# RWKV layer: the decays' products alternate between the two halves of the rows, and the scan's gram products run head by head in a fixed order

## The chip, the cores and the metric

The kernel runs on one core of one Trainium2 chip. Its engines work side by side: TensorE (matmuls, PE in the profile; PEld is its weight loads), VectorE (DVE), ScalarE (ACT), GpSimd (POOL) and SyncE (SP), which here only issues DMA transfers. The metric is the device time of one execution in microseconds, and of several executions the median.

## The reference

Two decoder layers over 1024 positions of width 1024. Layer 0 mixes tokens with an RG-LRU, layer 1 with RWKV-7 time mixing; each has a cross-attention and a squared-ReLU MLP behind it. The change lies in layer 1's time mixing alone (16 heads of 64):

```python
xx = x_prev - x
r = (x + xx * mu[0]) @ w_rkv[0]
xw = x + xx * mu[1]
k = (x + xx * mu[2]) @ w_rkv[1]
v = (x + xx * mu[3]) @ w_rkv[2]
xa = x + xx * mu[4]
...
w_log = -jax.nn.softplus(-(w0 + jnp.tanh(xw @ w1) @ w2)) - 0.5
decay = jnp.exp(-jnp.exp(w_log))
a = jax.nn.sigmoid(a0 + (xa @ a1) @ a2)
...
def step(state, inp):
    r_t, w_t, k_t, v_t, a_t, b_t = inp
    sa = jnp.einsum('bhij,bhj->bhi', state, a_t)
    state = (state * w_t[:, :, None, :] + sa[..., None] * b_t[:, :, None, :]
             + v_t[..., None] * k_t[:, :, None, :])
    y_t = jnp.einsum('bhij,bhj->bhi', state, r_t)
    return state, y_t
```

The scan over positions is computed in 16 chunks of 64 positions: products within a chunk are matmuls, and only the state goes from chunk to chunk.

## The kernel before

All large products are made in three matmuls of a split operand (`mm3`, lines 317 to 319: high x high, high x low, low x high), each of at most 128 x 512 outputs into one PSUM bank.

The order on each engine is made by a scheduler that simulates the program; code is not simply run in the order in which it is written. Two helpers narrow it: `self.line(name)` keeps everything issued under one name in the order of writing on each engine, and `self.behind()` puts what follows behind all that was given before. SP issues its transfers strictly in its own order, and each waits for its operands there.

The RWKV layer has these stages in the profile:
- The low-rank products, then eight turns of k products (`fphase` with `w_rkv[0, 1]`), one feature block f of 128 (two heads) each; the last turn has two. Beside turn i the decays of the next block are made by `decay(f)`: the rank-64 outputs for `w2` lie on rows 0 to 63, those for `a2` on rows 64 to 127 of the same tiles (`wa2`, `hwa`), so each of these matmuls uses one half of the rows. Both halves of the positions (`hf`) are made, so there are twelve 64-row matmuls of 512 columns for each f, and a tanh on ACT (L1266) takes each bank.
- Behind turn f, `gram(f)` makes products of the chunk's keys (L1341), masks them on DVE (L1342), and SP stores them (L1348, L1349). From two such blocks POOL solves triangular systems (`solve`, L1369 and L1371, q = 0, 1, 2; DVE has q = 3). `solve_store` copies a part on ACT (L1381) and SP stores both (L1382, L1383).
- The r products: `rwkv_make_mix` makes their inputs (ACT L1156, DVE L1159, then the split of L232 on ACT and L233 on DVE). Each weight block is loaded by SP (L248) and split in the same two lines. Then the v products, with the prefetch for the scan.
- The scan. Ahead of it, the grams, masks and keys of chunks 0 and 1. For chunk c: `values` (L1717, copied on ACT by L1719), `from_state` (L1729), `flip_out` of an earlier chunk (PE L1663, DVE L1668), `solved` (PE L1735, DVE L1737), `scan_gram(c + 1, 0)` (L1612), `update` (PE L1742, DVE L1744), `scan_keys` (L1636), the masks (DVE L1622) and `scan_gram(c + 1, 1)`, `output` (L1749), `post_norm(c - 1)` (DVE L1656), which the next chunk's `flip_out` reads. On POOL run `decayed` (L1724), `scan_scale` (L1602) and the power of `post_var` (L1651). Each of these functions runs under `self.line("scan")`, so their order among each other is fixed on each engine, and the order within one is the scheduler's.

A scan gram has eight matmuls, four head pairs q with two heads h. Head 0 has its operands on rows 0 to 63, head 1 on rows 64 to 127, and the two write to two banks. In the trace each shows as two passes, so 16 rows.

Of the kernel before, what the change touches and what calls it, by code (L numbers as in the profile page):

```python
# [1200 lines left out]
def rwkv(self, X, xt, lw_wa, lw_g, post):  # L1201
    nc, I = self.nc, self.I
    mm = nc.tensor.matmul
# [17 lines left out]
    wa2 = self.split(raw)  # L1221
    xk, xr, xv = ([[], []] for _ in range(3))
    for hf in range(2):
        o = hf * 512
        for lw, sh, hid in maps:
            ps = [self.bank() for _ in range(2)]
# [10 lines left out]
        if hf:  # L1237
            h = maps[0][2]
            nc.scalar.activation(h[0:64, :], h[0:64, :], AF.Tanh)
            hwa = self.split(h)  # L1240
        self.catch_up()
        rwkv_make_mix(self, X, 2, hf, xk[hf])
    h = maps[1][2]
# [10 lines left out]
    hr = [slice(0, 64), slice(64, 128)]  # L1254
    dk, st_k, mg, sol, ld, sm, xts = {}, {}, {}, {}, {}, {}, {}

    def decay(f):
        cs = slice(f * 128, f * 128 + 128)
        c1 = lambda t: t[:, f:f + 1]
        lw, a = self.unit(), self.unit()  # L1260
        for t, r, b in ((lw, slice(0, 64), self.w0h), (a, slice(64, 128), self.a0h)):
            for hf in range(2):
                s = slice(hf * 512, hf * 512 + 512)
                p = self.bank()
                self.mm3(p, (wa2[0][r, cs], wa2[1][r, cs]), (hwa[0][r, s], hwa[1][r, s]), True, True)
                nc.scalar.activation(t[:, s], p, AF.Tanh, bias=c1(b), scale=0.5)  # L1266
        nc.vector.tensor_scalar(lw, lw, -LC, -LC, ALU.mult, ALU.add)
        if f > 1:
            nc.scalar.activation(a, a, AF.Copy, scale=0.5, bias=0.5)
        else:  # L1270
            nc.vector.tensor_scalar(a, a, 0.5, 0.5, ALU.mult, ALU.add)
        IP = self.unit()
        nc.vector.tensor_tensor_scan(IP, d01, lw, 0.0, ALU.mult, ALU.add)
        P = lw
        nc.scalar.activation(P, IP, AF.Exp)
        nc.scalar.activation(IP, IP, AF.Exp, scale=-1.0)
        nc.sync.dma_start(Pd[cs, :], P)
        nc.scalar.copy(self.pc.rearrange("p (c q) -> p c q", q=8)[:, :, f], P[:, 63::64])
        dk[f] = a, P, IP
# [151 lines left out]

    self.depth, self.ahead = DA
    decay(0)
    for i, fs in enumerate(TURNS):
        for f in TURNS[i + 1] if i < 6 else []:
            decay(f)
        if len(fs) > 1:

            self.later.append(lambda: rwkv_make_mix(self, X, 0, 0, xr[0], range(2)))
        if i:  # L1440
            sums(fs[0] - 1)
        self.fphase(I["b_w_rkv"][0, 1], fs, xk, prep)
        if 0 < i < 6:
            gram(fs[0] - 1)
        aside(i)
# [158 lines left out]
    def scan_gram(c, g):  # L1604

        if c >= 16:
            return
        s = cst[c]
        s["pv", g] = [self.bank(h).rearrange("p (q w) -> p q w", q=4) for h in range(2)]
        for q in range(4):  # L1610
            for h in range(2):
                mm(s["pv", g][h][:, q, :], s["st"][g][hr[h], q].rearrange("p w t -> p (w t)"), s["mv"][hr[h], 4 * g + q],  # L1612
                   start=True, stop=True)

    def scan_mask(c, g):
        if c >= 16:
# [70 lines left out]
    for c in range(2):  # L1687
        scan_scale(c)
        for g in range(2):
            scan_gram(c, g)  # L1690
            scan_mask(c, g)
            scan_keys(c, g)
# [4 lines left out]
    for c in range(16):  # L1697
# [5 lines left out]
        s = cst[c]  # L1703
        sv, mv, pcc, xtc, pcs = s["sv"], s["mv"], s["pcc"], s["xt"], s["pcs"]
# [60 lines left out]
        if c:  # L1765
            todo += [(scan_gram, c + 1, 0)]
        if c < 15:
            todo += [(update, 0), (update, 1)]
        if c:
            todo += [(scan_keys, c + 1, 0), (scan_keys, c + 1, 1), (scan_mask, c + 1, 0), (scan_gram, c + 1, 1), (scan_mask, c + 1, 1)]  # L1770
# [6 lines left out]
        if c > 4 and c % 2:  # L1777

            n = (c - 3) // 2
# [8 lines left out]
    w = I["b_w_o"][0]  # L1788
# [54 lines left out]
```

## Time and profile before

| | |
|---|---|
| time, median of 3 runs | 2927.56 us (2922.16 to 2934.81) |
| span of the profiled execution | 2923.2 us |
| mean granted TensorE clock | 0.988 |
| 64-row matmuls of the decays, L317 to L319 | 32 each, 13.6 + 11.7 + 11.7 us busy |
| scan grams, L1612 | 512 passes, 47.4 us busy |

The profile gives no time of its own for the profiled execution beside its span, which runs from the first instruction to the last; the three runs shown lie from 1.0 us below it to 11.6 us above.

In rows of the order of time, the first two numbers are the start in us from the span's start and the duration of the (merged) row, then come engine, line, operation, output<-inputs by their tiles' names without numbers, sizes and a count; in brackets stands how long the engine had been idle and whose work ended that. A row of several instructions lasts from the start of the first to the end of the last. Matmuls are pipelined, so rows overlap by the part of a matmul that is only its way through the array.

### The profile page before, as it was taken

How to read it: one execution, taken by the hardware profiler on the slowest of the kernel's cores; microseconds unless marked ns; L12 is line 12 of the kernel's file. 1: busy time of each engine (PE TensorE's matmuls, PEld its weight loads, DVE VectorE, ACT ScalarE, POOL GpSimd, SP SyncE). 2: the span in 40 equal slices, each digit the busy share in tenths (PEclk: the TensorE clock that was granted, in tenths of full speed). 3: DMA queues.
4: the chain of work that ended last, by engine and by line, in shares of the span. 5: the costliest groups of instructions: out<-in, count | busy, mean ns of one | idle time of the engine just before them, and what ended most of it. 6: DMA issues, size and time to landing. Idle time of an engine off the chain costs nothing.

```text
span 2923.2 us, 42715 instructions
## 1 busy us (share of the span) xinstructions
PE 2828.6 (97%) x17051; PEld 2357.6 (81%) x17051; DVE 1758.2 (60%) x1935; ACT 1370.4 (47%) x2127; POOL 844.2 (29%) x930
## 2 busy tenths in 40 slices
PE   7999999999999999999999999999999999999998
PEld 6888798887888888887878677888788788888886
DVE  5577552457455577886675624773355645557778
ACT  6465342445444643448561534553244644454333
POOL 2000110023666500012288113751002366650001
PEclk9999999999999999999999999999999999999999
DMA  8212362123445554442657798952312344464443
GB/s 260 77 44 73 107 196 89 44 80 101 146 157 159 209 195 151 151 132 85 176 137 212 218 233 234 239 138 99 94 58 80 101 157 147 147 238 163 157 173 115
DMA packets 383591, 421.92 MB, mean 144 GB/s; under 512 B 91184, under 2 KB 294176, under 8 KB 383392
## 3 DMA queue, kind: packets, MB, share of 16 engines
q1 hardware_dynamic: 371360, 379.19, 42.8%
q0 software_dynamic: 11568, 39.41, 3.7%
q8 instruction: 134, 2.20, 0.3%
q14 instruction: 65, 0.53, 0.1%
q10 hardware_dynamic: 464, 0.59, 0.1%
HBM read 283.79 MB, written 134.74 MB: 143 GB/s over the span
## 4 chain that ended last, share of the span: by engine, by line
PE 87%; DVE 5%; DMA 3%; ACT 2%; issue 2%; SPq 1%; POOL 0%; DVEq 0%; POOLq 0%; ACTq 0%
PE q L317 15%; PE q L319 15%; PE q L318 15%; PE p L317 12%; PE p L319 11%; PE p L318 11%; DVE u L233 2%; PE q L1612 1%; DMA u<-d 1%; DMA u<-in_b_w_rkv 1%; ACT u L232 1%; PE q L1505 1%; DVE u L1159 0%; PE q L1729 0%; PE q L358 0%
## 5 line engine op out<-in xcount | busy, mean ns | idle before, releaser
L233 DVE TENSOR_TENSOR u<-u,u 128x1024 fp32r<-128x1024 f32 (+1 forms) x550 | 740.1, 1377 | 358.2 <-ACT u L232 336.0
L232 ACT CAST u<-u 128x1024 fp32r<-128x1024 f32 (+1 forms) x550 | 542.0, 1022 | 400.8 <-DVE u L1002 224.7
L317 PE MATMUL q<-u,u 128*128 128x512 f32 (+2 forms) x1824 | 698.0, 385 | 9.8 <-ACT u L232 7.5
L318 PE MATMUL q<-u,u 128*128 128x512 f32 (+2 forms) x1824 | 697.2, 383 | 1.1 <-POOL u L365 0.5
L319 PE MATMUL q<-u,u 128*128 128x512 f32 (+2 forms) x1824 | 691.7, 383 | 0.5 <-DVE u L233 0.5
L317 PE MATMUL p<-u,u 128*128 128x512 f32 (+1 forms) x1728 | 658.3, 383 | 21.7 <-ACT u L232 9.5
L318 PE MATMUL p<-u,u 128*128 128x512 f32 (+1 forms) x1728 | 656.0, 380 | 6.5 <-DVE u L233 6.5
L319 PE MATMUL p<-u,u 128*128 128x512 f32 (+1 forms) x1728 | 653.0, 378 | 3.2 <-DVE u L233 3.2
L328 POOL TENSOR_SCALAR s<-s 128x1 f32<-128x1 f32 x98 | 38.5, 393 | 1449.0 <-ACT u L326 1429.7
L317 PEld LDWEIGHTS q<-u,u 128*128 128x128 f32 (+1 forms) x1824 | 343.2, 189 | 80.6 <-ACT u L232 9.2
L317 PEld LDWEIGHTS p<-u,u 128*128 128x128 f32 x1728 | 330.0, 191 | 86.7 <-ACT u L232 14.9
L318 PEld LDWEIGHTS q<-u,u 128*128 128x128 f32 (+1 forms) x1824 | 343.5, 188 | 68.8 <-DVE u L233 2.8
L319 PEld LDWEIGHTS q<-u,u 128*128 128x128 f32 (+1 forms) x1824 | 343.4, 188 | 67.4 <-DVE u L233 0.7
L318 PEld LDWEIGHTS p<-u,u 128*128 128x128 f32 x1728 | 330.7, 191 | 68.8 <-DVE u L233 10.2
L319 PEld LDWEIGHTS p<-u,u 128*128 128x128 f32 x1728 | 329.8, 191 | 64.0 <-DVE u L233 4.9
L1060 DVE TENSOR_TENSOR z<-z,q 128x512 f32<-128x512 f32 x192 | 130.3, 682 | 81.2 <-PE q L319 81.2
L430 POOL TENSOR_TENSOR u<-u,u 128x512 f32<-128x512 f32 x96 | 150.9, 1575 | 8.3 <-PE q L318 5.1
L319 PE MATMUL q<-z,u 128*128 128x512 f32 x256 | 99.9, 390 | 1.2 <-DVE u L233 1.2
L318 PE MATMUL q<-z,u 128*128 128x512 f32 x256 | 99.6, 389 | 0.0
L317 PE MATMUL q<-z,u 128*128 128x512 f32 x256 | 99.3, 389 | 0.0
L639 DVE SCALAR_TENSOR_TENSOR u<-p,s,u 128x1024 f32<-128x1024 f32 x24 | 30.8, 1284 | 109.9 <-ACT u L232 62.4
L326 ACT ACTIVATE u<-u 128x1024 f32<-128x1024 f32 x58 | 61.4, 1061 | 74.1 <-DVE u L780 50.9
(252 smaller groups left out, 3254.8 us busy)
## 6 DMA issues: line engine op xcount, KB each, us to landing
u<-d SPq DMA_DIRECT2D x198, 512.0 KB, 4.6
d<-u SPq DMA_DIRECT2D x109, 512.0 KB, 3.4
d<-u POOLq DMA_DIRECT2D x68, 512.0 KB, 3.2
d<-u SPq DMA_DIRECT2D x132, 256.0 KB, 3.4
u<-in_m_w_up SPq DMA_DIRECT2D x64, 512.0 KB, 5.4
u<-in_m_w_down SPq DMA_DIRECT2D x64, 512.0 KB, 8.5
u<-in_c_w_kv SPq DMA_DIRECT2D x32, 512.0 KB, 7.0
u<-d SPq DMA_DIRECT2D x56, 256.0 KB, 7.4
```

Source lines behind the costliest of these rows:

```text
L232: self.nc.scalar.copy(hv, src)
L233: (eng or self.nc.vector).tensor_tensor(lv, src, hv, ALU.subtract)
L317: mm(o, ah, bh, start=first, stop=False, **kw)
L318: mm(o, ah, bl, start=False, stop=False, **kw)
L319: mm(o, al, bh, start=False, stop=last, **kw)
L326: nc.scalar.activation(junk, src, AF.Square, accum_out=ss)
L328: nc.gpsimd.tensor_scalar(v, ss, 1.0 / n, eps, ALU.mult, ALU.add)
L430: sub = lambda o, x, y: nc.gpsimd.tensor_tensor(o, x, y, ALU.subtract)
L639: nc.vector.scalar_tensor_tensor(o, src, r, gb, ALU.mult, ALU.mult)
L1060: nc.vector.tensor_add(to_, to_, o)
L1505: mm(pt[:, i * 128:i * 128 + 128], vt[:, tt * 128:tt * 128 + 128], self.center, start=True, stop=True)
L1612: mm(s["pv", g][h][:, q, :], s["st"][g][hr[h], q].rearrange("p w t -> p (w t)"), s["mv"][hr[h], 4 * g + q], start=True, stop=True)
```

## The change

`decay` now makes, for each half of the positions, both products at once: the bank of rows 0 to 63 and the bank of rows 64 to 127 take turns, matmul by matmul, and `line("decay")` keeps that order. The two activations follow. In `scan_gram` the eight matmuls stand under `line("gram")`, which keeps the order in which they are written: head 0, head 1, head 0 and so on.

```diff
-        for t, r, b in ((lw, slice(0, 64), self.w0h), (a, slice(64, 128), self.a0h)):
-            for hf in range(2):
-                s = slice(hf * 512, hf * 512 + 512)
-                p = self.bank()
-                self.mm3(p, (wa2[0][r, cs], wa2[1][r, cs]), (hwa[0][r, s], hwa[1][r, s]), True, True)
+        for hf in range(2):
+            s = slice(hf * 512, hf * 512 + 512)
+            ps = [self.bank() for _ in range(2)]
+            for n, (i, j) in enumerate(((0, 0), (0, 1), (1, 0))):
+                for p, r in zip(ps, hr):
+                    with self.line("decay"):
+                        mm(p, wa2[i][r, cs], hwa[j][r, s], start=n == 0, stop=n == 2)
+            for t, p, b in zip((lw, a), ps, (self.w0h, self.a0h)):
                 nc.scalar.activation(t[:, s], p, AF.Tanh, bias=c1(b), scale=0.5)
...
         for q in range(4):
             for h in range(2):
-                mm(s["pv", g][h][:, q, :], s["st"][g][hr[h], q].rearrange("p w t -> p (w t)"), s["mv"][hr[h], 4 * g + q],
-                   start=True, stop=True)
+                with self.line("gram"):
+                    mm(s["pv", g][h][:, q, :], s["st"][g][hr[h], q].rearrange("p w t -> p (w t)"), s["mv"][hr[h], 4 * g + q],
+                       start=True, stop=True)
```

Lines behind the first edit move down by 3, those behind the second by 4: L1381 becomes L1384, L1612 becomes L1616, L1622 L1626, L1656 L1660, L1717 L1721.

On PE, the second half of the positions of one feature block (f = 3) reads in the difference of the two orders like this; q_10760 is before the change a bank of rows 64 to 127, as q_10765 is, and after it a bank of rows 0 to 63 beside q_10761 of rows 64 to 127, and p_10785 is a k product:

```order
-L317 MATMUL q_10760<-u_10405,u_10080 128x512
-L318 MATMUL q_10760<-u_10406,u_10080 128x512
-L319 MATMUL q_10760<-u_10405,u_10081 128x512
-L317 MATMUL q_10765<-u_10405,u_10080 128x512
-L318 MATMUL q_10765<-u_10406,u_10080 128x512
-L319 MATMUL q_10765<-u_10405,u_10081 128x512
+L1267 MATMUL q_10760<-u_10405,u_10080 128x512
 L318 MATMUL p_10785<-u_10295,u_10521 128x512
 L319 MATMUL p_10785<-u_10294,u_10522 128x512
+L1267 MATMUL q_10761<-u_10405,u_10080 128x512
+L1267 MATMUL q_10760<-u_10406,u_10080 128x512
+L1267 MATMUL q_10761<-u_10406,u_10080 128x512
```

The two banks alternate now, and the first matmul stands apart, with two full matmuls between it and the rest. Before, a feature block's twelve matmuls stood in one or two runs of one half after the other (14 runs in all, of 9, 3, 12, 12 and ten times 6); now there are 21.

On SP, at the end of the k products, before the change; u_11552 and u_11558 are weight blocks of the r products, d_10067 and d_10068 what `solve_store` stores of the first solve:

```order
L1330 DMA db<-d_11431 64x8 x4
L248 DMA u_11552<-in_b_w_rkv 128x8x128
L1301 DMA d_10064<-u_11134 64x1024 x2
L1302 DMA d_10064<-u_11419 64x1024 x2
L1298 DMA d_10063<-u_11416 128x1024
L248 DMA u_11558<-in_b_w_rkv 128x8x128
L1348 DMA d_10066<-u_11438 32x16x32 x2
L1349 DMA d_10065<-u_11438 512x1x32
...
L1382 DMA d_10067<-u_10908 128x1024
L1383 DMA d_10068<-u_10907 64x1024
```

And after it, where the first row is the second part of the gram's store:

```order
L1351 DMA d_10066<-u_11438 32x16x32 x2
L1352 DMA d_10065<-u_11438 512x1x32
L1385 DMA d_10067<-u_10908 128x1024
L1386 DMA d_10068<-u_10907 64x1024
L248 DMA u_11552<-in_b_w_rkv 128x8x128
L248 DMA u_11558<-in_b_w_rkv 128x8x128
```

Both loads stand behind the two stores of the first solve now. The readers keep their place: ACT casts u_11552 right behind the copy of L1381 and the cast of the block before, in both orders.

On DVE, in one of the scan's chunks before the change; u_14660 and u_14675 are the masked grams of the next chunk, u_14354 the output that `post_norm` scales:

```order
L1744 TENSOR_TENSOR u_14248<-u_14242,q_14568 64x256 x2
L1622 TENSOR_TENSOR u_14660<-q_14617,mask 128x4x128
L1622 TENSOR_TENSOR u_14660<-q_14618,mask 128x4x128
L1622 TENSOR_TENSOR u_14675<-q_14666,mask 128x4x128
L1656 TENSOR_TENSOR u_14354<-u_14354,g_14586 128x512
L1622 TENSOR_TENSOR u_14675<-q_14665,mask 128x4x128
```

And after it:

```order
L1748 TENSOR_TENSOR u_14248<-u_14242,q_14568 64x256 x2
L1626 TENSOR_TENSOR u_14660<-q_14617,mask 128x4x128
L1626 TENSOR_TENSOR u_14660<-q_14618,mask 128x4x128
L1626 TENSOR_TENSOR u_14675<-q_14665,mask 128x4x128
L1626 TENSOR_TENSOR u_14675<-q_14666,mask 128x4x128
L1660 TENSOR_TENSOR u_14354<-u_14354,g_14586 128x512
```

All four masks stand ahead of the norm now. This is so in six chunks; in the others they stood so before. On PE, the first gram of a scan chunk alternated between the heads before too, by the scheduler's choice, and the second one, as the four ahead of the scan, ran four of one head and then four of the other; now all alternate. POOL's order is the same.

## The prediction

> **What bounds the kernel now.** I read the page first, then the busy time by stretches, then the order of time around each edited place. The time is the sum of one core's run: the profiled execution spans 2923.2 us, the three runs shown have a median of 2927.56, so I add 4.4 us to a span to compare it with them, and carry differences over one to one.
>
> ```profile
> span 2923.2 us, 42715 instructions
> PE 2828.6 (97%) x17051; PEld 2357.6 (81%) x17051; DVE 1758.2 (60%) x1935; ACT 1370.4 (47%) x2127; POOL 844.2 (29%) x930
> ```
>
> TensorE is busy 97% of the span, so a kernel that spends less time in matmuls looks like a sure gain. But the share is an average, and the two edits sit in stages that have to be asked one by one.
>
> ```profile
> 1376.00:1480.00 104.00, 104.00 (x701) 82.41 (x700) 67.67 (x63) 64.68 (x85) 36.69 (x44) 1.00 0.58 163
> 1498.30:1539.00 40.70, 36.31 (x246) 29.17 (x245) 40.21 (x38) 29.48 (x41) 36.06 (x37) 0.99 0.40 108
> 1539.00:1620.00 81.00, 79.78 (x678) 65.39 (x680) 43.61 (x64) 15.72 (x20) 54.60 (x91) 0.96 0.72 206
> 1806.00:1938.00 132.00, 129.80 (x2678) 117.31 (x2676) 97.98 (x186) 76.85 (x326) 102.83 (x118) 0.99 0.98 224
> ```
>
> The columns are the stretch, its length, the busy time of PE, PEld, DVE, ACT and POOL, the granted clock, the DMA share and GB/s. The decays stand in the first stretch, the k products, where PE never rests. The second is the change from k to r products: there DVE is busy 40.21 of 40.70 us, so DVE sets the pace. The last is the scan, where PE is busy almost throughout, which does not yet say who waits for whom.
>
> **The decays on PE.** A run of six 64-row matmuls on the same half, between full ones, and a place where the scheduler of before happened to let two halves meet:
>
> ```profile
> 1412.37 0.39 PE L317 MATMUL p<-u,u 128*128 128x512 f32 x1
> 1412.68 0.50 PE L317 MATMUL q<-u,u 64*128 64x512 f32 x1
> 1413.02 0.39 PE L318 MATMUL q<-u,u 64*128 64x512 f32 x1
> ...
> 1413.95 0.39 PE L319 MATMUL q<-u,u 64*128 64x512 f32 x1
> 1414.26 0.50 PE L318 MATMUL p<-u,u 128*128 128x512 f32 x1
> 1414.60 0.40 PE L319 MATMUL p<-u,u 128*128 128x512 f32 x1
> ```
>
> ```profile
> 1385.35 0.51 PE L318 MATMUL q<-u,u 64*128 64x512 f32 x2
> 1385.58 0.51 PE L319 MATMUL q<-u,u 64*128 64x512 f32 x2
> ```
>
> From 1413.02 to 1413.95 are four steps: 0.23 us a matmul, whatever its rows. From 1412.37 to 1414.60 are 2.23 us; without the run it would be two steps, 0.46, so six matmuls cost 1.77, and 1.77 - 6 x 0.23 = 0.39 us is lost at the two ends of the run, where PE goes from 128 rows to 64 and back. The x2 rows hold one matmul of each half and follow each other in 0.23 us: a pair of halves costs one step. Now count by the order. Before: 14 runs, which take 6 + 3 + 9 + 9 + 10 x 6 = 87 steps (nine pairs overlap already). After: the first matmul of many groups is split off by one or two full ones, so there are 21 runs (7, 5, 1, 11, 1, 11 for the first three features, then 6, 1, 5 three times, 6, 6 once and 1, 5, 1, 5), 56 steps in all. That is (87 - 56) x 0.23 = 7.1 us less streaming and 7 x 0.39 = 2.7 us more at the ends of runs: **PE's k products end 4.4 us earlier**. Up to the first gram of the third feature, on which the first solve waits, it is nine steps less and two runs more, 1.3 us.
>
> **What that 4.4 us meets.** The next stage starts with these rows:
>
> ```profile
> 1495.22 2.08 ACT L1381 COPY u<-u 64x1024 f32<-64x1024 f32 x1 [10.79 <-POOL u L1371]
> 1497.20 1.99 ACT L232 CAST u<-u 128x1024 fp32r<-128x1024 f32 x2
> 1498.28 2.36 DVE L233 TENSOR_TENSOR u<-u,u 128x1024 fp32r<-128x1024 f32 x2 [9.07 <-ACT u L232]
> 1507.84 1.22 DVE L1286 TENSOR_TENSOR u<-u,p 128x1024 f32<-128x1024 f32 x1 [0.45 <-ACT u L1285]
> ```
>
> ACT stands 10.79 us for POOL's first solve, DVE 9.07 us for ACT, and then DVE works without a rest to 1539. PE's end of the k products is late for that chain by 0.45 us only (L1285 evacuates its last product). So of the 4.4 us, 0.45 counts by itself, and 1.3 because the solve starts that much earlier. The rest is idle time of PE.
>
> The change also moves SP's queue. Before:
>
> ```profile
> 1483.75 0.59 SPq L248 DMA_DIRECT2D u<-in_b_w_rkv  x1
> 1498.50 0.48 SPq L1383 DMA_DIRECT2D d<-u  x1
> DMA to landing us min/median/max: 4.2/4.8/7.9
> ```
>
> The load of u_11552 is issued at 1483.75. After, by the order, it stands behind the two stores of the first solve, and the second of these is the row at 1498.50, which waits for the ACT copy that ends at 1497.30. So it is issued at about 1497.9 (0.6 for the store). The third row is the landing time of the eleven loads of these weights from 1376 to 1560: 4.8 us in the median. The second of the two casts at 1497.20 reads u_11552; it began near 1498.15 and would begin at 1497.9 + 4.8 = 1502.7, 4.55 us later. ACT's mixes for r stand behind it, DVE's second L233 waits for it, and DVE's chain behind that. No other work covers this: DVE has no slack to 1539. Bounds: 4.2 and 7.9 give 3.95 and 7.65; I take the median row. **Net: 4.55 - 1.3 - 0.45 = 2.8 us later** (2.2 to 5.9). In the stretch to 1620 PE is busy 79.78 of 81.00, so what is late at 1539 stays late. The other transfers that move in the queue (the next load of these weights, the stores of the last k feature and of the solve) are read behind the mixes or later; I cost them nothing, and up to 1 us if that cover is gone. That the tanh activations now come in the order of the halves too is hidden by PE, since ACT is busy 64.68 and DVE 67.67 of the 104 us.
>
> **The grams ahead of the scan.** Four runs of 16 gram passes stand here; alternating saves about 0.55 us each (below), 2.2 in all. Behind them:
>
> ```profile
> 1802.84 2.08 PE L1612 MATMUL q<-z,u 64*128 64x128 f32 x16 [4.68 <-issue]
> 1802.91 1.04 POOL L1602 TENSOR_TENSOR u<-u,pc 128x512 f32<-128x512 f32 x1 [6.58 <-DMA u<-d]
> 1776.03 2.44 SPq L1512 DMA_DIRECT2D u<-u  x4
> 1796.28 6.13 SPq L1558 DMA_DIRECT2D u<-d  x4
> ```
>
> PE stands 4.68 us for the operands of the next gram, and POOL, which reads the same loads, names the DMA. The two SP rows are the first and the last of six that follow each other without a gap: SP issues at its own pace from 1776 to 1802. 2.2 us earlier on PE is 2.2 us more of that wait: **nothing**.
>
> **The scan.** One chunk, with a gram that alternates already by the order of before (first row) and one that doesn't (second):
>
> ```profile
> 1824.76 1.16 PE L1612 MATMUL q<-z,u 64*128 64x128 f32 x16
> 1827.98 1.71 PE L1612 MATMUL q<-z,u 64*128 64x128 f32 x16
> 1832.06 0.63 PE L1663 MATMUL q<-ident,u 128*128 128x128 f32 x4 [0.21 <-DVE u L1656]
> 1834.78 1.16 PE L1612 MATMUL q<-z,u 64*128 64x128 f32 x16
> 1826.58 1.77 DVE L1744 TENSOR_TENSOR u<-u,q 64x256 f32<-64x256 f32 x4 [0.29 <-PE q L1742]
> 1828.38 2.48 DVE L1622 TENSOR_TENSOR u<-q,mask 128x512 f32<-128x512 f32 x4
> 1830.78 1.14 DVE L1656 TENSOR_TENSOR u<-u,g 128x512 f32<-128x512 f32 x1
> 1830.33 2.49 POOL L1602 TENSOR_TENSOR u<-u,pc 128x512 f32<-128x512 f32 x2
> ```
>
> The same 16 passes take 1.16 us alternating and 1.71 us half after half: 0.55 us to win in each of 13 chunks. (The Trainium skill, "TensorEngine Tiling (Array Packing)", section "Theoretical Speedup", allows up to twice the speed for two tiles of 64 rows. By it the gain would be 0.85 us a chunk, an estimate from that page; these rows show 1.47 times, and they decide.) But look at L1663. It waits for DVE's L1656, which follows the updates and four masks without a rest: 1826.58 to 1832.06 is 5.48 us from the first update to L1663, and from there PE's next pieces up to the next update, none of them an edited gram, take (1834.78 - 1832.06) + (1826.58 - 1824.76) = 4.54. 5.48 + 4.54 = 10.02, just the chunk's 1834.78 - 1824.76. A faster gram only lengthens the 0.21 us of that wait. In every second chunk of before L1656 stands ahead of the fourth mask, PE does not wait, and the chunk is shorter:
>
> ```profile
> 1814.98 1.16 PE L1612 MATMUL q<-z,u 64*128 64x128 f32 x16
> 1840.21 0.76 DVE L1656 TENSOR_TENSOR u<-u,g 128x512 f32<-128x512 f32 x1
> 1836.61 1.77 DVE L1744 TENSOR_TENSOR u<-u,q 64x256 f32<-64x256 f32 x4 [0.29 <-PE q L1742]
> 1836.14 1.65 POOL L1651 TENSOR_TENSOR g<-g,nhalf 128x8 f32<-128x8 f32 x1
> 1825.98 1.65 POOL L1651 TENSOR_TENSOR g<-g,nhalf 128x8 f32<-128x8 f32 x1
> ```
>
> 1824.76 - 1814.98 = 9.78, a pair 19.80. The order of after has L1656 behind four masks in all of them, six chunks more than before. L1656 takes 1.14 where POOL's L1602 began first (1830.33 against 1830.78) and 0.76 where it didn't. After a chunk in which L1663 waited, POOL's chain stands 1836.61 - 1836.14 = 0.47 ahead of the update instead of 1826.58 - 1825.98 = 0.60, so L1602 lets go 0.13 later: a chunk of 10.15 when all wait. Six pairs: 6 x (20.30 - 19.80) = **3.0 us longer**; with 10.02 it is 1.4.
>
> **Sum**: + 2.8 + 0 + 3.0 = 5.8 us on 2923.2, a span of 2929.0, and 2927.56 + 5.8 = 2933 for the time. Inside half a per cent (14.6 us), about what a measurement of this kernel can tell from no change.
>
> **Rivals.** *PE rules after all*: its busy share speaks for it. Then the decays' 4.4 and seventeen grams' 0.55 (9.3) all count, 13.7 us, 2914. Against it stand the three waits above, for POOL, DMA and DVE: 0.12. *DVE comes first to L1656*: if the scan's faster PE shifts POOL so that L1656 begins before L1602, it takes 0.76, the chunk is 10.02 - 0.38 = 9.64, six pairs 6 x (19.28 - 19.80) = - 3.1, and with + 2.8 the time is 2927. The rows at 1830 speak against it by 0.45 us, and 0.3 in a row of waiting chunks: 0.22. (The Trainium skill, "SBUF — State Buffer", section "SBUF: two separate sides", calls the port pair that DVE and GpSimd share an exclusive lock that whoever starts first keeps for the whole instruction. By it the price is all or nothing, as the two durations of L1656 show; if they shared it evenly, 10.02 would fall by part of the 0.38.) *The late load lands last*: issued with the solve's stores beside it, it lands in 7.9 us, 3.1 more than I took; PE then idles past 1510, and a low-clock stretch like the one in 1539 to 1620 (0.96 of 81 us, 3.2 us lost) comes on top. It decides once the load lands after about 1505. 5.8 + 3.1 + 3.2 = 12.1, 2940: 0.16. *The pairs don't overlap*: then 96 steps in 21 runs, 2.1 + 2.7 = 4.8 longer in the k products, and more ahead of r; the x2 rows all but exclude it: 0.02. The forecast keeps 0.48.
>
> **How the numbers follow.** The range reaches from 2920, below the second rival with some microseconds for the spread of the runs (2922.16 to 2934.81), to 2943, above the late load; it leaves most of the first rival out. Faster by over 0.5% (under 2912.9) is about a third of the first rival, 0.05; slower (over 2942.2) a third of the late load and a little of the forecast, 0.07; the rest, 0.88, is within.
>
> **What would show it.** Right: the k products' 64-row matmuls in pairs, PE idle for some microseconds before the r products, the second cast behind L1381 (a few lines further down after the edit) 4 to 6 us behind the first, named by a DMA; gram runs of 1.16 everywhere; L1663 waiting in every chunk, 0.8 us instead of 0.2 in half of them; chunks of 10.0 to 10.2. Wrong: chunks of 9.6 or 9.3, or a cast that doesn't wait.

## The result, and the profile after

The changed kernel takes 2936.63 us (median of 16 runs, 2930.93 to 2941.96), the kernel before 2928.97 (16 runs beside them). That is 7.7 us more; the ratio is 1.003, with a 95% interval from 1.0023 to 1.0037. 2933 was forecast, in a range from 2920 to 2943. The profiled execution has a span of 2934.0 us.

The page of after, with the same two lines as before:

```profile
span 2934.0 us, 42717 instructions
PE 2825.6 (96%) x17051; PEld 2352.0 (80%) x17051; DVE 1761.8 (60%) x1935; ACT 1372.1 (47%) x2127; POOL 844.5 (29%) x930
```

TensorE does work 3.0 us less, and the span is 10.8 us longer. The busy time by stretches (k products, change to r, scan; the columns are the stretch, its length, the busy time of PE, PEld, DVE, ACT and POOL, the granted clock, the DMA share and GB/s):

```profile
1378.00:1485.00 107.00, 104.39 (x722) 80.06 (x722) 66.45 (x64) 64.00 (x84) 40.63 (x50) 0.97 0.56 158
1506.50:1552.00 45.50, 37.15 (x237) 29.77 (x236) 44.34 (x40) 29.51 (x41) 42.36 (x41) 0.92 0.34 88
1813.00:1946.00 133.00, 126.52 (x2676) 112.61 (x2672) 100.75 (x185) 78.17 (x326) 103.17 (x118) 0.99 0.97 222
```

In each of them PE is now idle for longer than in its counterpart before: 2.6, 8.4 and 6.5 us where it was 0, 4.4 and 2.2. The clock fell in the first two (0.97 and 0.92, where it was 1.00 and 0.99). Now the places one by one, in the order of time.

**The k products.** One feature whose pairs run as forecast, and one whose pairs don't:

```profile
1407.30 0.97 PE L1267 MATMUL q<-u,u 64*128 64x512 f32 x6
...
1450.27 0.50 PE L1267 MATMUL q<-u,u 64*128 64x512 f32 x1
1453.38 0.96 PE L1267 MATMUL q<-u,u 64*128 64x512 f32 x5 [2.62 <-DVE u L1345]
...
1454.92 0.77 PE L317 MATMUL p<-u,u 128*128 128x512 f32 x1
```

Six matmuls in 0.97 us are three steps: the pairs overlap. At 1450.27 the first matmul of a pair runs, and the second, which writes to the other bank, waits 2.62 us for DVE's L1345, the mask of the gram that still holds that bank. From 1454.6 on PE has half its clock for 6.8 us (granted clock 0.50; the full matmul behind the short ones takes 0.77, where it took 0.49 before). Before, the matmul that first needed such a bank was the fourth of its run and not the second, and started 0.1 us late. PE comes to this place 2.7 us sooner than before (1450.27 against 1451.23, and the stage began 1.7 us later), but the mask only 0.5 us sooner (1452.64 against 1451.39), because the change of order also split the four small transfers that it needs. SP's queue before:

```profile
1442.59 1.12 SPq L1301 DMA_DIRECT2D d<-u  x2
...
1446.20 3.67 SPq L1330 DMA_DIRECT2D db<-d  x4
```

And after, with the mask on DVE:

```profile
1442.35 1.87 SPq L1333 DMA_DIRECT2D db<-d  x2
1444.31 1.19 SPq L1304 DMA_DIRECT2D d<-u  x2
...
1448.04 2.45 SPq L1333 DMA_DIRECT2D db<-d  x2
1452.64 1.29 DVE L1345 TENSOR_TENSOR u<-q,db 128x512 f32<-128x512 f32 x2 [6.74 <-DMA db<-d]
```

Two of the four go out first and two behind the feature's stores.

**From k to r.** ACT, SP's queue, the landing of the four weight loads between 1440 and 1530, and PE:

```profile
1496.09 2.12 ACT L1384 COPY u<-u 64x1024 f32<-64x1024 f32 x1 [6.00 <-POOL u L1374]
1498.11 1.04 ACT L232 CAST u<-u 128x1024 fp32r<-128x1024 f32 x1
1506.58 1.05 ACT L232 CAST u<-u 128x1024 fp32r<-128x1024 f32 x1 [7.42 <-DMA u<-in_b_w_rkv]
1491.08 1.34 SPq L1305 DMA_DIRECT2D d<-u  x2
...
1497.83 0.58 SPq L1352 DMA_DIRECT2D d<-u  x1
1498.51 0.66 SPq L1385 DMA_DIRECT2D d<-u  x1
1499.28 0.48 SPq L1386 DMA_DIRECT2D d<-u  x1
1499.85 2.60 SPq L248 DMA_DIRECT2D u<-in_b_w_rkv  x2
DMA to landing us min/median/max: 4.4/6.7/7.0
1517.57 0.76 PE L317 MATMUL p<-u,u 128*128 128x512 f32 x1 [5.14 <-DVE u L1289]
```

This is the forecast wait, 7.42 us long: the second cast names the load that was moved behind the stores, and PE stands 5.14 us ahead of the r products.

**Ahead of the scan and in it.** The first scan gram still waits for the same DMA, and then two chunks:

```profile
1810.11 1.23 PE L1616 MATMUL q<-z,u 64*128 64x128 f32 x8 [4.87 <-DMA u<-d]
...
1832.68 1.16 PE L1616 MATMUL q<-z,u 64*128 64x128 f32 x16
1835.91 1.64 PE L1616 MATMUL q<-z,u 64*128 64x128 f32 x16
1840.12 0.63 PE L1667 MATMUL q<-ident,u 128*128 128x128 f32 x4 [0.41 <-DVE u L1660]
1842.84 1.16 PE L1616 MATMUL q<-z,u 64*128 64x128 f32 x16
1846.07 1.16 PE L1616 MATMUL q<-z,u 64*128 64x128 f32 x16
1850.19 0.65 PE L1667 MATMUL q<-ident,u 128*128 128x128 f32 x4 [0.66 <-DVE u L1660]
1838.39 2.49 POOL L1605 TENSOR_TENSOR u<-u,pc 128x512 f32<-128x512 f32 x2
1838.71 1.27 DVE L1660 TENSOR_TENSOR u<-u,g 128x512 f32<-128x512 f32 x1
PE q L1667 <- DVE u L1660: 5.7, 11, 0.7
```

A chunk is 1842.84 - 1832.68 = 10.16 us, and the last row, from the waits between 1813 and 1946, says that L1667 now waits for the norm in 11 chunks, 5.7 us in all. The second gram takes 1.16 us in every other chunk only; in the rest it is 1.64, and the third pass, the first that belongs to the other head and writes to the other bank, begins at 1836.42, 0.51 us behind the first pass. The profile names nothing there. It begins right behind DVE's last update (which ends at 1836.28), so a second bank is again the likely cause, but this is read from times alone.

### The profile page after: what moved, and what is told of

Same layout as the page of the kernel before. It is cut to its first block, busy times and chain, and to the rows that moved or that the text cites. A ratio compares the mean times of both kernels' runs of the same rounds, so it can differ in the third digit from the quotient of the medians.

```text
span 2934.0 us, 42717 instructions
## 1 busy us (share of the span) xinstructions
PE 2825.6 (96%) x17051; PEld 2352.0 (80%) x17051; DVE 1761.8 (60%) x1935; ACT 1372.1 (47%) x2127; POOL 844.5 (29%) x930
## 4 chain that ended last, share of the span: by engine, by line
PE 83%; DVE 6%; DMA 4%; ACT 2%; issue 2%; SPq 2%; POOL 1%; DVEq 0%; POOLq 0%; ACTq 0%
PE q L319 15%; PE q L317 15%; PE q L318 15%; PE p L317 11%; PE p L319 11%; PE p L318 11%; DVE u L233 2%; DMA u<-d 2%; DMA u<-in_b_w_rkv 1%; DVE u L1626 1%; ACT u L232 1%; DVE u L1159 1%; PE q L1616 1%; PE q L1267 1%; PE q L1508 0%
## 5 line engine op out<-in xcount | busy, mean ns | idle before, releaser
L317 PE MATMUL q<-u,u 128*128 128x512 f32 (+1 forms) x1792 | 684.1, 384 | 9.8 <-ACT u L232 7.5
L318 PE MATMUL q<-u,u 128*128 128x512 f32 (+1 forms) x1792 | 685.5, 383 | 1.4 <-DVE u L233 0.8
L319 PE MATMUL q<-u,u 128*128 128x512 f32 (+1 forms) x1792 | 680.2, 382 | 0.5 <-DVE u L233 0.5
L317 PEld LDWEIGHTS q<-u,u 128*128 128x128 f32 x1792 | 337.9, 189 | 75.8 <-ACT u L232 8.9
L318 PEld LDWEIGHTS q<-u,u 128*128 128x128 f32 x1792 | 338.0, 189 | 67.9 <-DVE u L233 2.4
L319 PEld LDWEIGHTS q<-u,u 128*128 128x128 f32 x1792 | 337.9, 189 | 66.2 <-DVE u L233 0.7
```

Source lines behind the costliest of these rows:

```text
L317: mm(o, ah, bh, start=first, stop=False, **kw)
L318: mm(o, ah, bl, start=False, stop=False, **kw)
L319: mm(o, al, bh, start=False, stop=last, **kw)
```

## The experiments

All runs were made with kernels of before beside them on the same chip. What each run changes is told in the sections below the table. "Over before" is the difference to the median of before in the same call (before runs again in each call, and its medians lie between 2926.3 and 2929.0); the interval of the ratio of the two stands behind it. The next three columns are read from each profile: us from the first 64-row matmul of the decays to the sixth and to the ninth run of the solves' grams (PE L1341 or its successor: the end of the k products, and the r products under way), and the sum of the twelve chunks from the seventh of the scan's gram runs to the thirty-first.

| kernel | median us | over before | 95% interval of the ratio | to 6th gram | to 9th gram | 12 chunks |
|---|---|---|---|---|---|---|
| before | | | | 133.9 | 194.6 | 120.3 |
| the change | 2936.63 | +7.7 | 1.0023 to 1.0037 | 136.0 | 199.8 | 121.1 |
| decay_alone | 2933.62 | +5.7 | 1.0013 to 1.0038 | 135.8 | 200.4 | 122.3 |
| gram_alone | 2928.62 | +0.7 | 0.9994 to 1.0015 | 133.9 | 193.9 | 121.2 |
| both_store6 | 2934.93 | +7.0 | 1.0017 to 1.0039 | 136.1 | 196.1 | 121.2 |
| both_norm_first | 2927.51 | -0.5 | 0.9986 to 1.0011 | 135.4 | 201.3 | 115.8 |
| both_load_first | 2929.76 | +2.0 | 0.9998 to 1.0020 | 135.5 | 194.8 | 121.1 |
| both_db_first | 2932.82 | +5.1 | 1.0004 to 1.0023 | 130.0 | 198.3 | 121.1 |
| gram_norm_first | 2922.24 | -5.5 | 0.9970 to 0.9994 | 133.8 | 191.6 | 119.3 |
| norm_first_alone | 2926.27 | -1.5 | 0.9984 to 1.0003 | 134.1 | 191.7 | 121.0 |
| all_three | 2920.78 | -5.6 | 0.9971 to 0.9991 | 129.7 | 191.2 | 114.5 |
| all_three_store6 | 2921.12 | -5.2 | 0.9970 to 0.9990 | 129.8 | 186.0 | 116.0 |
| gram_norm_store6 | 2923.00 | -3.3 | 0.9980 to 0.9999 | 134.0 | 191.3 | 115.9 |
| all_three_pool_copy | 2919.68 | -8.5 | 0.9953 to 0.9977 | 129.7 | 183.9 | 119.8 |

The last three columns come from one profile each. before, gram_alone, gram_norm_first and norm_first_alone run the same instructions up to the ninth gram, and that column has 191.6 to 194.6 for them: a difference of 3 us there says nothing.

The theories: A, the forecast's own (a late load behind the solve, and DVE's order in the scan); B, TensorE rules; C, which the profile of after suggested, that the decays' wait for a second bank and the half clock behind it are what costs.

### The two edits apart

decay_alone has the first hunk of the diff, gram_alone the second.

> The decay edit without the gram edit. Theory A (the late weight load): the load of the second weight block of the r products stands behind the two stores of the first solve, as in the full change; its cast waits 6 to 8 us and the r products begin 4 to 6 us later than before against the start of the stage, so the time is 4 to 6 us over before, about 2934. Theory B (TensorE rules): the decays end 4.4 us earlier and so does the kernel, about 2925. Theory C (the second bank): with the late load aside, what counts is that the first product of a pair must wait for two free banks; TensorE stands about 2.6 us in the decays of the sixth feature and runs a low-clock stretch behind it, and the k products' end is what is late: 3 to 5 us, with no idle time left before the r products.

> The gram edit without the decay edit. Theory A (DVE's order in the scan): all chunks 10.0 to 10.2 us, each with a wait of 0.4 to 0.8 for the norm ahead of the transposes, 3 us over before, about 2932; the stages ahead of the scan as before. Theory B (TensorE rules): 17 x 0.55 = 9 us less, about 2920.

Measured: +5.7 and +0.7 us. B falls for both. In decay_alone the load lands later still:

```profile
1509.65 1.05 ACT L232 CAST u<-u 128x1024 fp32r<-128x1024 f32 x1 [8.56 <-DMA u<-in_b_w_rkv]
```

gram_alone has the chunks of theory A, 10.1 to 10.17 us where nothing disturbs them, but its median is only 0.7 over before. Its interval (1.8 us under before to 4.4 over) holds 0 and the 3 us alike. The decays cause most of the loss. A and C are still open for them.

### The norm ahead of the second masks

```diff
-            todo += [..., (scan_mask, c + 1, 0), (scan_gram, c + 1, 1), (scan_mask, c + 1, 1)]
+            todo += [..., (scan_mask, c + 1, 0), (post_norm, c - 1), (scan_gram, c + 1, 1), (scan_mask, c + 1, 1)]
         todo += [(output,)]
-        if c:
-            todo += [(post_norm, c - 1)]
```

both_norm_first has it on the change, gram_norm_first on gram_alone, norm_first_alone on before.

> The full change, with the scan's norm given ahead of the second pair of masks on VectorE. Theory A (the place of the norm sets the chunk): the transposes of flip_out wait no more, and the next limit is the last mask or TensorE: chunks of 9.2 to 9.5 us instead of 10.13, 7 to 11 us less than the full change, 2926 to 2930. Rival (VectorE's sum of work sets the chunk, wherever the norm stands): chunks stay above 10.0, 2936.

> The gram edit alone, with the scan's norm ahead of the second pair of masks, and the decays as before. Chunks as in the full change with the norm first, 9.4 and 9.7 us in turn, a mean of 9.55 where before had 9.9: 4 to 6 us under before, 2922 to 2924.

> Before, with the scan's norm ahead of the second pair of masks, and no alternation. If TensorE sets the chunk once the norm is out of the way, the slow second gram counts: 9.37 + 0.55 = 9.9 in one parity and 9.7 + 0.07 = 9.8 in the other, about as before, 2926 to 2928; the alternation is then worth 3 to 5 us beside the moved norm and nothing without it. Rival (VectorE's place of the norm is all there is): chunks of 9.55 without any alternation, 2923.

The same places of both_norm_first:

```profile
1832.26 1.64 PE L1616 MATMUL q<-z,u 64*128 64x128 f32 x16
1835.99 0.66 PE L1667 MATMUL q<-ident,u 128*128 128x128 f32 x4
1838.73 1.16 PE L1616 MATMUL q<-z,u 64*128 64x128 f32 x16
1841.96 1.16 PE L1616 MATMUL q<-z,u 64*128 64x128 f32 x16
1848.11 1.16 PE L1616 MATMUL q<-z,u 64*128 64x128 f32 x16
1833.86 0.68 DVE L1660 TENSOR_TENSOR u<-u,g 128x512 f32<-128x512 f32 x1
```

L1667 has no bracket any more: it waits for nothing. Undisturbed chunks are 9.37 and 9.70 us in turn, the 0.33 between them the slower second gram. PE sets the pace now, and L1660 takes 0.68 us instead of 1.27, since it begins ahead of POOL's L1605. Theory A holds: 8.1 us less than the change, each taken over before in its own call. And the alternation begins to pay: without it (norm_first_alone, chunks of 9.77 where undisturbed) the moved norm gives -1.5 us, with it -5.5. So the grams are worth about 4 us once nothing waits for the norm (two kernels of one call, whose intervals overlap), and nothing that shows while something does.

### ScalarE's copy one step later

```diff
-SL, SO, ST = (2, 5, 8, 9), (2, 5, 8, 9), (5, 8, 12, 13)
+SL, SO, ST = (2, 5, 8, 9), (2, 5, 8, 9), (6, 8, 12, 13)
```

> The full change, with the copy and the stores of the first solve given one step later, so that ScalarE does not stand for GpSimd's solve ahead of the casts for r, and SyncE issues the late load ahead of those stores (by the order it then stands behind the gram's stores, at about 1498.5 instead of 1499.85). Theory A (late load behind the solve): the second cast begins 1.3 us earlier or more, the first one 8 us earlier; the time falls by 1.3 to 5 us against the full change, 2931 to 2935. Theory C (k's end is what is late): no change, 2937.

```profile
1491.02 1.04 ACT L232 CAST u<-u 128x1024 fp32r<-128x1024 f32 x1
1504.90 1.05 ACT L232 CAST u<-u 128x1024 fp32r<-128x1024 f32 x1 [12.84 <-DMA u<-in_b_w_rkv]
```

Against the first decay the first cast comes 8 us earlier than in the change and the second 2.6, and the second still waits for the load, which SP issues at 1499.19. The ninth gram comes 3.7 us earlier than in the change, but hardly any of it is left at the end (7.0 over before). The merge of the first solve now waits for stores that are later (its PE line waits 3.6 us for DMA, where it was 2.2). The time lies at the upper end of what A gave, and doesn't exclude C.

### The load first, and the small transfers together

both_load_first holds back the stores that stood ahead of the loads; both_db_first does the same with the stores of one feature, so that the four transfers into `db` stay together.

```diff
+        if f == 6:
+            with (self.tc.issue_after(self.wload) if not self.rec else ExitStack()):
+                while late:
+                    nc.sync.dma_start(*late.pop(0))
...
-        nc.sync.dma_start(MVd[:, f, 0, :], at)
+        store(f, 5, MVd[:, f, 0, :], at)
```

`store(f, at, ...)` puts a transfer on the list `late` where f is at; it is used for the sixth feature's stores (f = 5), for those of the fifth feature's gram (f = 4) and of the first solve, and `wload` is the last weight load. both_db_first holds back the stores of the fourth feature (f = 3), in a list that `gram` empties behind the transfers into `db`.

> The full change, with the stores of the sixth k feature, of its gram and of the first solve given behind the two weight loads, so that SyncE's queue has the loads directly behind the small transfers of the norms (as before the change, and some 13 us ahead of where the full change has them). Theory A (the late load): the second cast begins right behind the first, at most 1 us of wait; from the sixth gram to the ninth TensorE takes 60 to 61 us as before, where the full change took 63.9; the time is 3 to 4 us under the full change, 2932 to 2934, and what is left over before is the scan's and 2 us of the k products' end. Theory C (the k products' end is what is late, by the wait for a second bank): no change, 2936 to 2937.

> The full change, with the four small transfers of the norms of the third gram together again, ahead of the stores of the fourth feature. The second decay of the pair then finds its bank free about 1.2 us earlier: its wait falls from 2.6 to 1.4 us or less, and the low-clock stretch behind it may go. Theory C (this wait and its low clock are what the decays cost): the sixth gram begins 1 to 4 us earlier and the time falls as much, 2932 to 2935. Theory A (late load): TensorE only stands longer ahead of the r products (5.1 us in the full change), the time stays at 2936 to 2937.

both_load_first, SP and ACT, and PE's wait for the bank; then both_db_first, PE and SP, and its wait ahead of the r products:

```profile
1490.40 1.16 SPq L248 DMA_DIRECT2D u<-in_b_w_rkv  x2
1499.51 2.00 ACT L232 CAST u<-u 128x1024 fp32r<-128x1024 f32 x2
PE q L1269 <- DVE u L1359: 2.3, 1, 2.3
```

```profile
1449.42 1.31 PE L1267 MATMUL q<-u,u 64*128 64x512 f32 x6
1443.77 3.28 SPq L1336 DMA_DIRECT2D db<-d  x4
PE p L317 <- DVE u L1291: 8.2, 1, 8.2
```

With the load early both casts run on end, and the ninth gram comes at 194.8 us as before the change (194.6), although the wait for the bank (2.3 us) and the half clock behind it are still there. The time falls to 2.0 over before. With the transfers together, the bank is free in time (six matmuls without a bracket), no half clock follows, and the sixth gram comes at 130.0: 6 us earlier than in the change and 3.9 earlier than before. But PE then stands 8.2 us instead of 5.1 ahead of r, and the ninth gram gains 1.5 us.

**The late load is the larger part of what the decays cost**: with the load early, 5.7 of the 7.7 us are gone, more than the 3 to 4 that A gave, though the sixth gram comes as late as in the change. C is real as a wait; what it costs is less plain. The time of both_db_first, 2932.8, is the one that C gave and not A's 2936 to 2937. That its interval and the change's meet at 1.0023 is no sign of equal times: the ratios lie 0.0016 apart, which is 4.7 us, and the differences of the medians 2.6. But the edit moved the load too: SP issues it 1.1 us sooner (1500.18 - 1375.80 = 124.4 us behind the first decay, where the change has 125.5), and the second cast begins 2.1 us sooner (130.1 and 132.2). So this run alone doesn't part C from A. What TensorE's 4 us are worth there is left to the next section.

### All of it, and what the decays are worth

all_three has the norm, the load and the transfers repaired; all_three_store6 the later copy too; gram_norm_store6 is gram_norm_first with the later copy, without the decay edit.

> The full change with all three repairs: the weight loads ahead of the stores, the four small transfers of the norms together, the scan's norm ahead of the second pair of masks. Against gram_norm_first (2922.2), which has no decay edit, this shows what the alternating decays are worth once their two side effects are away. Theory A (ScalarE's copy behind GpSimd's solve sets the start of the r products): the sixth gram begins 4 us earlier than before the change, TensorE stands that much longer behind it, from the first decay to the ninth gram 193 to 194.5 us as before (194.6); the time 2921 to 2923. Theory B (TensorE rules there): 4.4 us less, about 2918.

> all_three, and the copy and the stores of the first solve one step later, so that ScalarE's casts for r wait for nothing from GpSimd. If that copy was the limit: the r products begin right behind the k products, from the first decay to the ninth gram 187 to 189 us instead of 194, and the time falls by 3 to 7 us against all_three, 2915 to 2919; the merge of the first solve may wait up to 2.6 us for its later stores (as it did in both_store6) and give part of it back. If not: 2921 to 2923.

> gram_norm_first (no decay edit) with the copy and the stores of the first solve one step later. With the r products begun right behind the k products, TensorE sets the pace there: from the first decay to the ninth gram 191 to 192 us, the time 2919 to 2921, and all_three_store6 then shows the decays' 4 us below it. If the alternating decays are worth nothing even then, the two are equal.

all_three is 5.6 us under before, gram_norm_first 5.5: with both side effects gone the alternating decays give nothing that shows, as A said (two calls; by the two intervals, 4 to 5 us either way are not excluded). Its sixth gram comes 4.1 us earlier than gram_norm_first's, its ninth 0.5 (191.2, where 193 to 194.5 was expected). With the copy out of the way the ninth comes at 186.0 with the decay edit and at 191.3 without it, so there PE's time does count. Yet all_three_store6 ends where all_three does, not 3 to 7 us below it: that expectation missed. So did the one of gram_norm_store6: it takes 2923.0 us where 2919 to 2921 was expected, and all_three_store6 lies 1.9 us below it and not 4, which is within the spread. Where the gain goes isn't shown. The merge waits 4.0 us for DMA instead of 2.2, but the stretch from the ninth gram to the first scan gram is as long in the one profile as in the other (216.7 and 217.0 us), and the profiled execution of all_three_store6, 2915.84, is the fastest of its twelve.

all_three_pool_copy is meant to take the copy off ACT without holding back the stores: it lets POOL make the copy, right behind its solve, and leaves the stores in their place:

```diff
+        if not q:
+            nc.gpsimd.tensor_copy(L[0:64].rearrange(...), xt_[0:64].rearrange(...))
...
-        nc.scalar.copy(L[0:64].rearrange(...), xt_[0:64].rearrange(...))
+        if q:
+            nc.scalar.copy(L[0:64].rearrange(...), xt_[0:64].rearrange(...))
```

> all_three, with the copy of the first solve's result made by GpSimd behind its own solve instead of by ScalarE, and its stores where all_three has them (not 16 us later as in all_three_store6). ScalarE then waits for nothing from GpSimd ahead of its casts for r. If that wait is what swallows the decays' 4 us: from the first decay to the ninth gram 186 to 188 us, as in all_three_store6 (186.0), and without the late merge more of it is left at the end: 2914 to 2919. If GpSimd's copy delays its second solve, or another wait follows, 2920 to 2922 as all_three (2920.8) and all_three_store6 (2921.1).

```profile
1489.33 1.05 ACT L232 CAST u<-u 128x1024 fp32r<-128x1024 f32 x1 [2.40 <-DMA u<-in_b_w_rkv]
1496.62 1.35 POOL L1390 TENSOR_TENSOR w<-u,u 128x135 f32<-128x135 f32 x1
1502.70 2.08 POOL L1400 COPY u<-u 64x1024 f32<-64x1024 f32 x1
PE q L1432 <- DMA u<-d: 6.3, 2, 6.0
```

The casts run at 1489 and the ninth gram comes at 183.9, 10.7 us earlier than before. It is the fastest of all, 8.5 us under before (6 runs beside 10). Against all_three, whose interval overlaps, that is 3 us more by the medians and not clear of the spread; 2919.7 lies at the border of the two times that were expected. What the profile shows of the loss: POOL's steps are slower while DVE works (1.35 us for one that took 0.48 before the change, when DVE stood), its solve ends 126.3 us behind the first decay instead of 122.5, and the merge then waits 6.0 us for what comes from it.

## Why the prediction was right, and what was mis-sized

- **The decays on PE: right.** A pair is one step, and the sixth gram comes 3.8 to 4.4 us earlier where nothing holds the pairs up (129.7 to 130.0 against 133.8 to 134.1). Forecast: 4.4.
- **What they meet: one wait was missing.** The prediction counted steps and not banks. A pair needs two free banks at its start, and of what moved on SP the prediction named the next load and the stores ("read behind the mixes or later; I cost them nothing") and not the transfers into `db`: two of these slid behind the stores, and the mask that frees the bank came with them. 2.6 us of waiting and 3.4 lost at half clock turned 4.4 us earlier into 2 us later. With the load early (both_load_first) 2.0 us are left over before, this wait and the scan's loss included, so it is the smaller part; its price by itself stays open, since both_db_first moved the load too.
- **The late load: right in kind, too small.** Forecast net 2.8 us; decay_alone measures 5.7. Its term was "4.55 - 1.3 - 0.45". Against the first decay the load was issued at 1499.85 - 1374.38 = 125.47, where the working had 1497.9 - 1.3 - 1372.67 = 123.93: 1.5 us later. Most of this was in the row that the prediction showed. It put the load 0.6 us behind the copy's end at 1497.30, but the second store is issued at 1498.50 for 0.48 us, so the load could not go out before 1498.98. SP is busy with stores almost without a gap from 1490 on, in the change as before it (L1386 at 1499.28, 1.1 us behind the copy's end). The rest is that ACT's copy came only 0.8 us earlier against the first decay and not 1.3. And the load landed 6.7 us later instead of 4.8, with the stores beside it. 2.8 + 1.5 + 1.9 = 6.2. The rival of the late load lay at 2940, with a landing of 7.9 and a further low-clock stretch. Both signs of it came in part: a landing of 6.7, and 5.0 us at half clock behind the wait at 1517.57. But DVE, which sets the pace there, was busy for all of the 7 us from 1517 on, so the half clock may have cost nothing; the time is nearer to the forecast.
- **The grams ahead of the scan: right, with the saving too large.** The four take 5.5 us instead of 6.8, 1.4 less and not 2.2. In gram_alone the wait behind them grows by as much, from 4.68 to 6.03 us, and names the DMA, so nothing comes of it. In the change it is 4.87.
- **The scan: right in kind, the sum too large.** The wait for L1660 is there in all chunks, and undisturbed chunks are 10.10 and 10.16 (forecast 10.0 to 10.2). But "six pairs, 3.0 us" compares undisturbed chunks. PE also stands now and then in the scan for other things, mostly for nothing that the profile names; before, this counts in full (1.5 us of the 120.3, by 6 x 19.80 = 118.8; in decay_alone, whose scan is the same, 3.5). In the five kernels that wait for the norm in every chunk they fall into that wait, and the twelve chunks add up to 121.1 or 121.2. So about 2 us of the 3 were already lost before. This is read from one profile of each kernel; the interval of gram_alone doesn't exclude 3.0. That gram runs are "1.16 everywhere" was wrong: every other second gram takes 1.64.
- **The rivals.** PE does not rule as long as these waits stand. Once the norm is out of the way it does in the scan (about -4 us for the grams). That DVE comes first to L1660 did not happen by itself, but it is what moving the norm brings about: 0.68 us, and 9.37 for the chunk.

The sum of +5.8 lies near +7.7 because one term was some 3 us too small and the other some 2 us too large: the mechanisms were right, the nearness of the sum is in part luck.

## What to carry to other kernels

Interleaving two half-array products shortens them on TensorE (here a pair of 512 columns took the 0.23 us of one, and sixteen gram passes 1.16 us instead of 1.71) and changes what they wait for: here the second matmul of a pair needed the bank that the fourth had needed before. Everything that the scheduler moves in answer has to be costed, too, the queues of small transfers first. Before making an engine's work shorter, look for who waits for whom at the end of that stage; here a copy behind another engine's solve, a queue of stores and the place of one norm decided, and whether the grams' saving counted hung on one norm that stood behind two masks. A share of 97% busy says little, since the idle time that a change brings need only be a few microseconds.

## What the runs showed of the hardware

- Short waits of TensorE can be enough for half clock: 2.62 us of idle at 1450 were followed by 6.8 us at 0.5, and 1.96 us in all_three by 3.1. Not each of them is: 1.83 us ahead of 1522.46 in before were followed by full clock. (The Trainium skill, "TensorE: Matmul & The Clock Gate", section "What's actually happening", has the clock fall after an idle window of about 3.4 us in windows that run on their own. The 6.8 us agree with two such windows; the 3.1 us, and the 5.0 us behind the longer wait at 1517.57, are only what is left of the half clock when work begins again. An idle time of a whole window wasn't needed here.)
- The pauses of PE without a named cause differ from run to run of the same instructions. In the stretch from the ninth gram to the first scan gram, the same up to there in before, gram_alone, gram_norm_first and norm_first_alone, PE paused 0.6, 4.2, 2.1 and 2.9 us ahead of one merge, and the stretch took 212.1, 212.5, 210.5 and 216.7 us. What it is stays open. One profile against another tells nothing below 5 us there, and only the medians do.
